# Gate projections in seven block products for eight, their tanh tiles kept in memory, the branch projections after all gates

## The chip, the cores and the metric

The kernel runs on one core of one Trainium2 chip, as one program. The metric is the device time of one execution in microseconds; where several executions were timed, the median stands for them. The core has a matrix engine (TensorE, in the profile PE, with PEld for its weight loads), a vector engine (VectorE, DVE), a scalar engine (ScalarE, ACT), a general engine (GpSimd, POOL) and a queue that issues all of this kernel's transfers (SyncE, SP). Each engine takes its instructions in the order in which they are written to it.

## The reference, cut to what matters

One decoder layer over 1024 positions of width 1024, in float32:

```python
h = rmsnorm(x, mix_norm)
q, k, v, su, sv, g_a, g_b = split(h @ w_in)
y_att = sliding_window_attention(q, k, v, ...)      # 8 heads of 64, window 128
y_sgu = gelu(su) * (tril(W_s) @ rmsnorm(gelu(sv)) + b)   # chunks of 128 positions
merged = sigmoid(g_a) * (y_att @ w_oa) + sigmoid(g_b) * (y_sgu @ w_ob)
x = x + merged @ w_out
z = causal_conv3(rmsnorm(x, ffn_norm) @ w_up)       # 2 * 2816 columns
x = x + (silu(z_gate) * z_val) @ w_down
```

`g_a` and `g_b`, the gate projections, are two products of `h` (1024 x 1024) with 1024 x 1024 weights.

## The kernel before, in words

Activations lie transposed: the feature is the partition, and the position is the free axis. Every operand of a product is split into a high part (a copy in the reduced format fp32r, made by ACT, `copy_hi`) and a low part (the rest, made by a subtraction on DVE or POOL). A product is then three matmuls: high by high, high by low, low by high. `mm3` (lines 74 to 76) writes them for dense products, `prod` (line 989) for block products.

The stages follow each other so:

1. x is loaded in eight feature tiles, and scaled and split into `hTh` and `hTl` (1024 positions in one piece from tile 2 on). The k and v projections run beside it.
2. The attention loop has 20 steps, each with hand-written places for the scores, the softmax, the transposes and the pv products, and with q, u and v-row matmuls as fillers (`FILL`). `pv_out` adds the two halves of a block's output and splits them into `yah` and `yal` (line 501).
3. The rest of the v rows (`pvs`): gelu, square and norm of each row, and its split into `vsh` and `vsl`. Here, and in the mixing products of the spatial gating unit (`sgu_mix`), a scheduler orders the instructions.
4. Gates and branches, as a list of jobs: 16 gate tiles of 48 matmuls (8 feature tiles, 2 halves, 3 products) and 16 branch tiles of 24. Jobs 0 to 2 are gates, then two gates and two branches alternate; the branches of tiles 6 and 7 come last. A gate's result is scaled, put through tanh(z/2) and held in SBUF (`th`, four buffers) until its branch multiplies it. Beside them run `sums_make` (line 825) and `sums_move`: these prepare the up projection, by loading the four quarter blocks of each pair of up weights, forming four sums, and storing all of them to memory.
5. Eight output tiles (`px`), which also split the next stage's operand into seven combinations.
6. The up projection in 22 pairs of tiles (`fast_pair`). A pair is a 2 by 2 block product in seven block products of 12 matmuls each (Winograd's form of Strassen's scheme), A11, S3, A12, S1, A22, S2, S4 by their partners. `Left` loads the weights p, q and r (r holds the sums S2 and S4, read back from memory), and splits them on ACT and POOL into `ph`/`pl`, `qh`/`ql`, `AX` and `s3h`/`s3l`. DVE forms u (line 1152), the two outputs, the scalings by the row norm, the convolution and the gated activation of the pair before; `x1` is a copy by ACT of the first product (line 1127), and the third product is added to the same PSUM bank after that copy.
7. The down projection in 7 block products of 11 slices, with the result written out.

SBUF's largest pool is `big`, with eight buffers of 16 KB per partition (`Y`). Its buffers pass from stage to stage: a new tile waits until the last reader of the old one is done. Weights come through three `raw` buffers. PSUM holds four tiles of 1024 columns (`PS`) in rotation.

Of the kernel before, what the change touches and what calls it, by code (L numbers as in the profile page):

```python
# [10 lines left out]
F = mybir.dt.float32  # L11
# [30 lines left out]
def body(ctx, tc, nc, a):  # L42
    base = ctx.enter_context(tc.tile_pool(name="base", bufs=1))
    big = ctx.enter_context(tc.tile_pool(name="big", bufs=8))
# [8 lines left out]
    def Y(s, dt=R, shape=None):  # L53
        return big.tile(shape or [128, 4, 1024], dt, tag="Y", name=nm(s))
# [40 lines left out]
    cp = base.tile([128, 186], F, name="cp")  # L95
# [26 lines left out]

    psA = ctx.enter_context(tc.tile_pool(name="psA", bufs=2, space=bass.MemoryType.PSUM, reuse_waits="tile"))
# [19 lines left out]
    hTh = [Y("hTh"), Y("hTh")]  # L143
    hTl = [Y("hTl"), Y("hTl")]
# [3 lines left out]
    def hh(k):  # L148
        return hTh[k // 4][:, k % 4, :]

    def hl(k):
        return hTl[k // 4][:, k % 4, :]
# [43 lines left out]
    xcuts = {0: (slice(0, 256), slice(256, 512), slice(512, 1024)), 1: (slice(0, 512), slice(512, 1024))}  # L196
    for k in range(8):
# [3 lines left out]
        for c in xcuts[k] if k in xcuts else (slice(0, 1024),):  # L201
            xc = x1[:, 257 + c.start:257 + c.stop]
            copy_hi(hh(k)[:, c], xc, scale=x1[:, 0:1])
            nc.vector.scalar_tensor_tensor(hl(k)[:, c], xc, x1[:, 0:1], hh(k)[:, c].bitcast(F),
                                           op0=ALU.mult, op1=ALU.subtract)
        for s in range(8):
            o = pkv[s // 4][:, (s % 4) * 256:(s % 4 + 1) * 256]
            c = slice(s * 128, (s + 1) * 128)
            mm3(o, hh(k)[:, c], hl(k)[:, c], wkv[:, 0, k, :], wkv[:, 1, k, :],
                k == 0 and s % 2 == 0, k == 7 and s % 2 == 1)  # L210
# [23 lines left out]
    def q_proj(n):  # L234
        half, b = divmod(n, 8)
        w = wq[half]
        p = PH("pq")[:, 0:256]
        c = slice(b * 128, (b + 1) * 128)
        for k in range(8):
            mm3(p, hh(k)[:, c], hl(k)[:, c], w[:, 0, k, :], w[:, 1, k, :], k == 0, k == 7)  # L240
        st[("pq", n)] = p
# [150 lines left out]
    yah, yal = Y("yah"), Y("yal")  # L392
    uT = Y("uT", F)
# [94 lines left out]
    def pv_out(n):  # L488
# [6 lines left out]
        for g in range(2):  # L495
            r = slice(64 * g, 64 * g + 64)
            nc.vector.tensor_tensor(o[r], p[r, g], o[r], op=ALU.add)
        ts_ = slice(2 * half, 2 * half + 2)
        cs = slice(b * 128, (b + 1) * 128)
        copy_hi(yah[:, ts_, cs], o)  # L500
        nc.vector.tensor_tensor(yal[:, ts_, cs], o, yah[:, ts_, cs].bitcast(F), op=ALU.subtract)
# [3 lines left out]
    def u_chunk(i):  # L505
# [4 lines left out]
        for k in (2 * j, 2 * j + 1):  # L510
            for h in range(2):
                c = slice(h * 512, (h + 1) * 512)
                mm3(p[:, c], wh[:, k, :], wl[:, k, :], hh(k)[:, c], hl(k)[:, c], k == 0, k == 7)
# [5 lines left out]
    def v_half(s, h):  # L519
# [3 lines left out]
        for k in range(8):  # L523
            mm3(pvs[s][:, 256 * h:256 * h + 256], hh(k)[:, c], hl(k)[:, c], wv[h][:, 0, k, :],
# [57 lines left out]

    assert "".join(FILL).count("u") == 16 and "".join(FILL).count("q") == 12
    man = tc.manual_schedule()
    man.__enter__()
    for n in range(20):
# [19 lines left out]
        weights(n)  # L606
        for t, p in u_done:
# [49 lines left out]

    sg_cm = tc.tile_pool(name="sg", bufs=1)
# [10 lines left out]
    with tc.issue_after(last_sel[0].ins):  # L669
# [4 lines left out]
    with tc.issue_after(last_exp[0].ins):  # L674
        for s in range(n_v[0], 4):
            v_half(s, 0)
        for s in range(8):
# [5 lines left out]
            p = pvs.pop(s)  # L683
            vg = sg.tile([128, 512], F, tag="vg", name=nm("vg"), bufs=2)
            nc.scalar.activation(vg, p, AF.Gelu_apprx_tanh, scale=rstd[:, s:s + 1])
            sq = sg.tile([128, 512], F, tag="vsq", name=nm("vsq"), bufs=1)
            ss = sg.tile([128, 1], F, tag="vss", name=nm("vss"), bufs=2)
            nc.scalar.activation(sq, vg, AF.Square, accum_out=ss)
            rsqrt_cols(ss, ss, 1, 512)
            nc.vector.scalar_tensor_tensor(vg, vg, ss[:, 0:1], sg_b, op0=ALU.mult, op1=ALU.mult)  # L690
            copy_hi(vsh[:, s, :], vg)
            nc.vector.tensor_tensor(vsl[:, s, :], vg, vsh[:, s, :].bitcast(F), op=ALU.subtract)

    psB.__exit__(None, None, None)
    psum["C"] = tc.tile_pool(name="psC", bufs=2, space=bass.MemoryType.PSUM, reuse_waits="tile")
    psC = psum["C"].__enter__()
    psum["P"] = [psC, psC, psA, psA]
    psum["H"] = None

    pools = {}  # L700
    yz = []

    def sgu_mix(t, half):
        y = yz[0]
# [13 lines left out]
        yv = y[:, t, 4 * half:4 * half + 4].rearrange("p s i -> p (s i)")  # L718
        nc.gpsimd.tensor_tensor(yv, yv, uT[:, t, 512 * half:512 * half + 512], op=ALU.mult)

    def sgu_close():
        ysh, ysl = Y("ysh"), Y("ysl")
        for t in range(4):
            yv = yz[0][:, t].rearrange("p s i -> p (s i)")
            copy_hi(ysh[:, t, :], yv)
            nc.vector.tensor_tensor(ysl[:, t, :], yv, ysh[:, t, :].bitcast(F), op=ALU.subtract)
        sg_cm.__exit__(None, None, None)
        zr_cm[0].__exit__(None, None, None)
        pools["ys"] = (ysh, ysl)
        pools["mg_cm"] = tc.tile_pool(name="mg", bufs=1)  # L730
        pools["mg"] = pools["mg_cm"].__enter__()
        pools["dr"] = ctx.enter_context(tc.tile_pool(name="dr", bufs=1, space=bass.MemoryType.DRAM))

    ms = [None] * 8
    th = {}
    jobs.clear()

    def gate(src, key):
        def main(w):
            p = PS("pg")  # L740
            dense(p, *w, hh, hl, 8)
            yield
            t = pools["mg"].tile([128, 1024], F, tag="th", name=nm("th"), bufs=4)
            nc.vector.tensor_tensor(t, p, rstd_b, op=ALU.mult)  # L744
            nc.scalar.activation(t, t, AF.Tanh, scale=0.5)
            th[key] = t
            sums_make()
            sums_move()
        jobs.append((src, 8, main))

    def branch(src, br, c):
        def main(w):
            yh, yl = (yah, yal) if br == "a" else pools["ys"]
            p = PS("po")
            dense(p, *w, lambda k: yh[:, k, :], lambda k: yl[:, k, :], 4)
            yield
            t = th.pop((br, c))
            if br == "b":
                ms[c] = pools["mg"].tile([128, 1024], F, tag=f"m{c}", name=f"m{c}")
                nc.vector.scalar_tensor_tensor(ms[c], t, 1.0, p, op0=ALU.add, op1=ALU.mult)  # L760
            else:
                nc.vector.scalar_tensor_tensor(t, t, 1.0, p, op0=ALU.add, op1=ALU.mult)
                nc.vector.tensor_tensor(ms[c], ms[c], t, op=ALU.add)
            if br == "b":
                sums_make()
                sums_move()
            if br == "b" and c == late[0]:
                mhi[:] = [Y("mh"), Y("mh")]
                mlo[:] = [Y("ml"), Y("ml")]
            for e in SPLITS.get((br, c), ()):  # L770
                m_split(e)
        jobs.append((src, 4, main))

    def m_split(c):
        copy_hi(mhi[c // 4][:, c % 4, :], ms[c])
        nc.vector.tensor_tensor(mlo[c // 4][:, c % 4, :], ms[c], mhi[c // 4][:, c % 4, :].bitcast(F),
                                op=ALU.subtract)

    mhi, mlo = [None, None], [None, None]
    late = (6, 7)  # L780
    SPLITS = {("b", 6): (0, 1, 2), ("a", 6): (3, 4), ("b", 7): (5, 6), ("a", 7): (7,)}
    gate(a["wgb"][0], ("b", 0))
    gate(a["wga"][0], ("a", 0))
    gate(a["wgb"][1], ("b", 1))
    for c in range(8):
        if c > 1:
            gate(a["wgb"][c], ("b", c))
        if c > 0:
            gate(a["wga"][c], ("a", c))
        if c not in late:  # L790
            branch(a["wob"][c], "b", c)
            branch(a["woa"][c], "a", c)

    sums = [0, None]

    def sums_move():


        i, last = sums
        if last:  # L800
            t = pools["dr"].tile([128, 4, 4, 128], F, tag=f"sum{i}", name=f"sum{i}")
            for h, (x, s3) in enumerate(last):
                ks = slice(2 * h, 2 * h + 2)
                nc.sync.dma_start(t[:, 1, ks], s3)
                nc.sync.dma_start(t[:, 0, ks], x[:, 1, 0])
                nc.sync.dma_start(t[:, 2:4, ks], x[:, 0])
# [639 lines left out]
```

## Time and profile before

| | us |
|---|---|
| median of three runs | 1255.4 (1251.83 to 1255.53) |
| the profiled execution | 1253.38 |
| its span in the profile | 1251.7 |
| TensorE busy in it | 1222.2 (98%) |
| VectorE busy | 879.7 (70%) |
| ScalarE busy | 493.5 (39%) |
| GpSimd busy | 423.9 (34%) |

The profile shows one execution. Times in it count from the span's start. A row of the timeline has the start, the duration, the engine, the line of the kernel, the operation and its tiles, and in brackets the engine's idle time before it with what ended that. A row of the windows has the busy time of each engine in a stretch, the granted TensorE clock, the share of the 16 DMA engines' time and GB/s.

### The profile page before, as it was taken

To read this page: it belongs to the slowest core of one execution; us is meant where nothing else is said; L and a number is where in the kernel's file an instruction comes from. 1 tells how busy PE (TensorE), PEld (TensorE's weight loads), DVE (VectorE), ACT (ScalarE), POOL (GpSimd) and SP (SyncE) were. 2 spreads that over 40 slices of the span, in tenths; PEclk is the share of its full clock that TensorE was granted. 3 is DMA by queue.
4 is the path that set the end of the run, shared out by engine and by line. 5 is a ranking of instruction groups with operands and counts; after the bars stand their busy time and mean duration, and the time that the engine had idled before them with its cause. 6 is when DMAs were issued, how large, how long until landed. Compare 5 with 4: busy or idle time off the path is not lost.

```text
span 1251.7 us, 16137 instructions
## 1 busy us (share of the span) xinstructions
PE 1222.2 (98%) x5962; PEld 1025.6 (82%) x5962; DVE 879.7 (70%) x1114; ACT 493.5 (39%) x773; POOL 423.9 (34%) x275
## 2 busy tenths in 40 slices
PE   7999999999999999899999999999999999999998
PEld 6878879988888888788778888888888888788887
DVE  8788896455555554767768777778777788776674
ACT  5665665421111112333434434344344353433332
POOL 5355566151222222233474354354354420000000
PEclk8999999999999999999999999999999999999999
DMA  5210003017777776535333443543533546985372
GB/s 210 82 51 19 17 18 93 1 45 247 238 238 242 244 248 225 200 118 177 126 110 138 165 150 105 175 151 126 176 125 129 176 160 201 400 276 195 116 230 87
DMA packets 114319, 194.97 MB, mean 156 GB/s; under 512 B 10944, under 2 KB 56256, under 8 KB 114240
## 3 DMA queue, kind: packets, MB, share of 16 engines
q1 hardware_dynamic: 114240, 193.94, 46.0%
q8 instruction: 47, 0.77, 0.3%
q14 instruction: 32, 0.26, 0.1%
HBM read 142.25 MB, written 51.64 MB: 155 GB/s over the span
## 4 chain that ended last, share of the span: by engine, by line
PE 79%; DVE 11%; issue 4%; DMA 2%; ACT 2%; POOL 2%; SPq 0%; POOLq 0%; DVEq 0%; ACTq 0%
PE pz L989 32%; PE pd L1268 9%; PE pdy L1268 7%; PE pg L75 4%; PE pg L74 4%; PE pg L76 4%; PE px L75 2%; PE px L76 2%; PE px L74 2%; PE po L75 2%; PE po L74 2%; PE po L76 2%; PE pvs L74 1%; PE pvs L75 1%; PE pvs L76 1%
## 5 line engine op out<-in xcount | busy, mean ns | idle before, releaser
L91 POOL TENSOR_TENSOR wjl<-wj,wjh 128x1024 fp32r<-128x1024 f32 (+1 forms) x40 | 82.9, 2074 | 231.0 <-ACT wjh L70 228.3
L70 ACT ACTIVATE wjh<-wj 128x1024 fp32r<-128x1024 f32 (+1 forms) x40 | 35.6, 889 | 211.2 <-PE pg L75 48.1
L825 DVE TENSOR_TENSOR ls<-ls 128x256 f32<-128x256 f32 x176 | 84.1, 484 | 36.0 <-DMA ls<-wup 29.4
L989 PE MATMUL pz<-T,qh 128*128 128x512 f32 x352 | 109.1, 391 | 0.0
L989 PE MATMUL pz<-B,ph 128*128 128x512 f32 x352 | 108.4, 389 | 0.0
L74 PE MATMUL pg<-hTh,wjh 128*128 128x512 f32 x256 | 99.6, 389 | 0.0
L75 PE MATMUL pg<-hTl,wjh 128*128 128x512 f32 x256 | 99.6, 389 | 0.0
L76 PE MATMUL pg<-hTh,wjl 128*128 128x512 f32 x256 | 99.6, 389 | 0.0
L954 POOL TENSOR_TENSOR s3l<-s,s3h 128x512 fp32r<-128x512 f32 x22 | 29.7, 1351 | 156.7 <-ACT s3h L70 156.7
L989 PEld LDWEIGHTS pz<-T,qh 128*128 128x128 f32 x352 | 66.3, 188 | 14.3 <-issue 0.5
L989 PEld LDWEIGHTS pz<-B,ph 128*128 128x128 f32 x352 | 66.1, 188 | 13.8
L744 DVE TENSOR_TENSOR th<-pg,rstd_b 128x1024 f32<-128x1024 f32 x16 | 19.6, 1225 | 77.8 <-PE pg L76 77.7
L994 ACT ACTIVATE tv<-pz,cp 128x1024 f32<-128x1024 f32 x22 | 26.6, 1207 | 108.0 <-DVE pz L1003 102.7
L954 POOL TENSOR_TENSOR ql<-wuq,qh 128x1024 fp32r<-128x1024 f32 x22 | 53.4, 2427 | 45.3 <-ACT qh L70 45.3
L989 PE MATMUL pz<-T,ql 128*128 128x512 f32 x176 | 68.5, 389 | 0.0
L1268 PE MATMUL pd<-bh,ah 128*128 128x512 f32 x176 | 68.5, 389 | 0.0
L1268 PE MATMUL pd<-bl,ah 128*128 128x512 f32 x176 | 68.5, 389 | 0.0
L989 PE MATMUL pz<-B,pl 128*128 128x512 f32 x176 | 68.5, 389 | 0.0
L1268 PE MATMUL pd<-bh,al 128*128 128x512 f32 x176 | 68.5, 389 | 0.0
L989 PE MATMUL pz<-T,AX 128*128 128x512 f32 x264 | 65.1, 396 | 1.0 <-DVE T L874 1.0
L989 PE MATMUL pz<-B,AX 128*128 128x512 f32 x264 | 63.4, 389 | 0.0
L989 PEld LDWEIGHTS pz<-T,AX 128*128 128x128 f32 x264 | 50.1, 191 | 11.9 <-DVE T L874 1.5
(298 smaller groups left out, 3481.3 us busy)
## 6 DMA issues: line engine op xcount, KB each, us to landing
ls<-wup SPq DMA_DIRECT2D x88, 256.0 KB, 3.5
sum<-ls SPq DMA_DIRECT2D x88, 128.0 KB, 2.2
sum<-ls SPq DMA_DIRECT2D x44, 256.0 KB, 2.3
wup<-wup SPq DMA_DIRECT2D x22, 512.0 KB, 3.9
wur<-sum SPq DMA_DIRECT2D x22, 512.0 KB, 5.2
ra<-wdown SPq DMA_DIRECT2D x44, 256.0 KB, 4.6
b<-T SPq DMA_DIRECT2D x44, 256.0 KB, 3.4
B<-tv SPq DMA_DIRECT2D x33, 256.0 KB, 2.0
```

The source lines that it names most:

```text
L70: return nc.scalar.activation(dst, src, AF.Copy, scale=scale)
L74: nc.tensor.matmul(out, wh, mh, start=first, stop=False)
L75: nc.tensor.matmul(out, wh, ml, start=False, stop=False)
L76: nc.tensor.matmul(out, wl, mh, start=False, stop=last)
L91: nc.gpsimd.tensor_tensor(l[:, :nk, :], r[:, :nk, :], h[:, :nk, :].bitcast(F), op=ALU.subtract)
L744: nc.vector.tensor_tensor(t, p, rstd_b, op=ALU.mult)
L825: nc.vector.tensor_tensor(o, p, q, op=op)
L954: nc.gpsimd.tensor_tensor(l, r, h.bitcast(F), op=ALU.subtract)
L989: nc.tensor.matmul(o, p[:, k, :], y[:, q, k, :], start=not more and k == 0 and j == 0, stop=k == 3 and j == 2, skip_group_check=True)
L994: nc.scalar.activation(t, z, AF.Identity, scale=cw[:, ci, 2:3], bias=cb[:, ci:ci + 1])
L1268: nc.tensor.matmul(o[d], p[:, k - k0, m], q[:, k - k0, :], start=new and k == 0 and j == 0, stop=k == HK - 1 and j == 2, skip_group_check= ...
```

## The change

It is one rewrite with these parts.

- The gate projections of feature tile c, `g_b` and `g_a`, become one pair (`gate_pair`) in the seven-product form of the up projection. A pair has 84 matmuls where its two gate tiles had 96. The seven combinations of x (`xb`: B11, B21, B22, T1 to T4) are formed once. B11, B21 and B22 are the quarter blocks of the split x that exist already, which is why x is now split in halves of 512 positions from tile 0 on (`hx`). For the four others x is loaded again (`rows_again`), scaled by ACT (`x_gain`), summed by DVE (`x_sums`) and split (`x_split`). The weights' sums S1 to S4 are formed on DVE (`sums_q`, `sums_r`).
- All gates come before all branches. The tanh tiles are stored to memory (`gate_out`) and loaded again two branches ahead (`th_load`). Branches run in the order b0 b1 a0 a1 b2 b3 a2 a3 and so on.
- The attention output `ya` is stored to memory unsplit, and loaded and split beside the last gate pairs (`ya_load`, `ya_split`). The spatial unit's output is split in the last pair (`ys_split`).
- From the v rows on everything is written in order by hand (`v_phase`). The first half of the mixing products moves in among the last v rows. Seven of the large buffers have tag Y, and one has a tag of its own, U.
- The up weights' sums stored ahead shrink to S3 and S1 (`sums_step`). In the up pairs S2 and S4 are formed by two DVE subtractions (`sums_r`) instead of being loaded, and their split (`split_r`) moves behind that of q.
- Job weights are loaded four jobs ahead instead of three.

The diff, cut to its core:

```diff
+    def x_gain(r, ks):
+        for k in ks:
+            x = xr_raw[r][:, k, :]
+            nc.scalar.activation(x, x, AF.Copy, scale=cp[:, 186 + 4 * r + k:187 + 4 * r + k])
...
+        if n == 15:
+            rows_again(0)
+        if n == 17:
+            x_gain(0, (0, 1))
+        if n == 18:
+            x_gain(0, (2, 3))
+            x_sums((0, 1), True)
+        if n == 19:
+            x_sums((2, 3), True)
...
+    rows_again(1)
...
-            job_load(i + 3)
+            job_load(i + 4)
...
+    X_WORK = {
+        0: lambda: g_left[0].split_p(),
+        1: lambda: x_gain(1, (0, 1)),
+        2: lambda: (x_gain(1, (2, 3)), x_sums((0, 1), False)),
+        3: lambda: x_sums((2, 3), False),
+        4: first_sums,
+    }
+    def v_phase():
...
+        g_left[0].load_p()
+        g_left[0].load_q()
...
+            if s > 0:
+                v_norm(s - 1)
+            if s > 5:
+                sgu_mix(s - 6, 0)
+            v_gelu(s)
+            if s in X_WORK:
+                X_WORK[s]()
+            v_rsqrt(s)
+            if s > 0:
+                v_split(s - 1)
...
+        def sums_r(self):
+            self.r = raw("lr")
+            s2 = sub(nc.vector, self.r[:, 0:4], self.q[:, 0:4], self.p[:, 0:4])
+            sub(nc.vector, self.r[:, 4:8], self.p[:, 4:8], s2)
...
+    def gate_out(key, z):
+        t = pools["ls"].tile([128, 1024], F, tag="th", name=nm("th"), bufs=3)
+        nc.scalar.activation(t, z, AF.Tanh, scale=0.5)
+        d = d_th[key] = pools["dr"].tile([128, 1024], F, tag=f"th{key}", name=nm("dth"))
+        nc.sync.dma_start(d, t)
...
+    def gate_pair(c, prev):
...
+        q.prod(q.g0, "A11", "B11")
...
+        nc.scalar.copy(x1, q.g0)
+        if prev:
+            gate_out(("b", c - 1), prev.zg)
+            sums_step()
+        else:
+            w.split_s3()
+            sgu_mul(0, 1)
+            x_split("T1")
+            w.split_q()
+            for t in (1, 2, 3):
+                sgu_mul(t, 1, nc.vector)
+            x_split("T4")
+            q.prod(q.g0, "A12", "B21", more=True)
+        q.prod(q.v0, "S3", "T3")
+        nc.scalar.copy(x7, q.v0)
+        if not c:
+            w.split_r()
+            x_split("T2")
+        else:
+            q.prod(q.g0, "A12", "B21", more=True)
+        if nx:
+            nx.sums_q()
+            nx.split_p()
+            nx.split_s3()
...
+        q.prod(q.g1, "S1", "T1")
+        nc.vector.tensor_tensor(x7, x7, q.g1, op=ALU.add)
+        if nx:
+            nx.sums_r()
...
+        q.prod(q.v0, "A22", "T4", more=True)
+        if nx:
+            nx.split_q()
...
+        q.prod(q.v1, "S2", "T2")
+        nc.vector.tensor_tensor(q.u2, x1, q.v1, op=ALU.add)
+        nc.vector.tensor_tensor(q.v0, q.u2, q.v0, op=ALU.add)
+        nc.vector.tensor_tensor(q.v1, q.u2, x7, op=ALU.add)
+        q.scale(q.zv)
...
+        gate_out(("a", c), q.zv)
+        q.prod(q.g1, "S4", "B22", more=True)
...
         prev.stores()
+        if nx:
+            nx.sums_r()
         if n + 2 < NPAIR:
             lefts[n + 2].load_p()
         q.prod(q.v0, "A22", "T4", more=True)
         if nx:
             nx.split_q()
+            nx.split_r(n + 1)
```

More of the change, by code (lines that the diff above doesn't have):

```diff
@@ L496, in pv_out @@
             r = slice(64 * g, 64 * g + 64)
[L497 to L501, printed above, removed]
+            nc.vector.tensor_tensor(ya[r, 2 * half:2 * half + 2, b * 128:(b + 1) * 128], p[r, g], o[r], op=ALU.add)
+        if b == 7:
+            for t in (2 * half, 2 * half + 1):
+                nc.sync.dma_start(d_ya[t], ya[:, t, :])
     ust = {("w", 0): tuple(u_next)}
@@ L682, in body @@
                 nc.scalar.activation(uT[:, s, :], uT[:, s, :], AF.Gelu_apprx_tanh)
[L683 to L700, printed above, removed]
+            if s > 0:
[8 more added lines that the diff above has]
+                v_split(s - 1)
+        v_norm(7)
+        v_split(7)
+        sgu_mix(2, 0)
+        sgu_mix(3, 0)
+    pools = {"dr": dr}
     yz = []
     def sgu_mix(t, half):
+        if not yz:
+            yz.append(Y("y", F, [128, 4, 8, 128]))
         y = yz[0]
@@ new lines, in body, with sums_load, sums_step @@
+    sums = {"load": 0, "make": 0}
+    def sums_load():
+        i = sums["load"]
+        if i < NPAIR:
+            x = pools["ls"].tile([128, 3, 4, 128], F, tag="ls", name=nm("ls"), bufs=2)
+            nc.sync.dma_start(x[:, 0], a["wup"][2 * i][:, 0:4])
+            nc.sync.dma_start(x[:, 1:3], a["wup"][2 * i + 1].rearrange("p (b k) m -> p b k m", b=2))
+            sums[i] = x
+            sums["load"] += 1
+    def sums_step():
+        i = sums["make"]
+        if i < NPAIR:
+            sums_load()
+            x = sums.pop(i)
+            sub(nc.vector, x[:, 0], x[:, 0], x[:, 1])
+            sub(nc.vector, x[:, 1], x[:, 1], x[:, 2], ALU.add)
+            t = pools["dr"].tile([128, 2, 4, 128], F, tag=f"sum{i}", name=f"sum{i}")
+            nc.sync.dma_start(t, x[:, 0:2])
+            pools.setdefault("sum", {})[i] = t
+            sums["make"] += 1
@@ new lines, in ya_split, with gates, th_load @@
+    def ya_split():
+        for t in range(4):
+            y_split("a", t, yb["raw"][:, t, :])
+    def gates():
+        q = None
+        for c in range(8):
+            q = gate_pair(c, q)
+        q.last_sum()
+        gate_out(("b", 7), q.zg)
+        gates_close()
+        for key in B_ORDER[:2]:
+            th_load(key)
+    B_ORDER = [(br, c + e) for c in range(0, 8, 2) for br in "ba" for e in (0, 1)]
+    ms = {}
+    def th_load(key):
+        th[key] = pools["ls"].tile([128, 1024], F, tag="th", name=nm("th"), bufs=3)
+        nc.sync.dma_start(th[key], d_th[key])
@@ L780, in body @@
[L780 to L806, printed above, removed]
-            pools.setdefault("sum", {})[i] = t.rearrange("p b k m -> p (b k) m")
-            i += 1
-        sums[:] = [i, None]
-        if i < NPAIR:
-            sums[1] = []
-            for h in range(2):
-                x = pools["mg"].tile([128, 2, 2, 2, 128], F, tag=f"ls{h}", name=nm("ls"))
-                s3 = pools["mg"].tile([128, 2, 128], F, tag=f"ls3{h}", name=nm("ls3"))
-                for t in range(2):
-                    nc.sync.dma_start(x[:, t], a["wup"][2 * i + t].rearrange("p (b k) m -> p b k m", b=2)
-                                      [:, :, 2 * h:2 * h + 2])
-                sums[1].append((x, s3))
@@ L840, in body @@
+    for n in range(16):
+        branch(n)
     comb = {}
@@ L1366, in body @@
     jobs.append((None, 0, None))
-    yz.append(zr[0].tile([128, 4, 8, 128], F, tag="Z", name="y"))
-    for i in range(3):
-        job_load(i)
-    job_split(0)
-    for half in range(2):
-        for t in range(4):
-            sgu_mix(t, half)
-    sgu_close()
-    with tc.manual_schedule():
-        job_split(1)
+    with tc.manual_schedule():
+        v_phase()
+        psB.__exit__(None, None, None)
+        psum["C"] = tc.tile_pool(name="psC", bufs=2, space=bass.MemoryType.PSUM, reuse_waits="tile")
+        psC = psum["C"].__enter__()
+        psum["P"] = [psC, psC, psA, psA]
+        psum["H"] = None
+        for t in range(4):
+            sgu_mix(t, 1)
+        x_split("T3")
+        for t in range(4):
+            sgu_mul(t, 0)
+        sg_cm.__exit__(None, None, None)
+        gates_open()
+        g_left[1].load_p()
+        gates()
         run_jobs()
```

359 lines of the change are left out of this document (221 added, 138 removed).

## The prediction

> **What bounds the kernel now.** I read the busy table, then the windows by stage, then TensorE's timeline.
>
> ```profile
> span 1251.7 us, 16137 instructions
> PE 1222.2 (98%) x5962; PEld 1025.6 (82%) x5962; DVE 879.7 (70%) x1114; ACT 493.5 (39%) x773; POOL 423.9 (34%) x275
> ```
>
> ```profile
> 200.00:237.00 37.00, 37.00 (x313) 37.00 (x312) 18.69 (x26) 19.05 (x36) 15.00 (x14) 1.00 0.21 65
> 237.00:256.00 19.00, 17.48 (x145) 17.10 (x144) 11.50 (x19) 5.91 (x12) 7.12 (x7) 1.00 0.00 1
> 256.00:500.00 244.00, 244.00 (x1081) 202.11 (x1080) 128.99 (x211) 45.15 (x49) 61.88 (x34) 1.00 0.68 221
> 640.00:1036.00 396.00, 396.00 (x1749) 327.90 (x1748) 306.15 (x313) 169.27 (x189) 169.75 (x81) 1.00 0.44 149
> ```
>
> TensorE (the first busy column) never rests in the gates and branches (256 to 500) or in the up pairs (640 to 1036). There only fewer matmuls, or a new wait, can change the time. A matmul's 389 ns is not its price, since its successor starts earlier:
>
> ```profile
> 329.92 0.39 PE L74 MATMUL pg<-hTh,wjh 128*128 128x512 f32 x1
> 332.64 0.39 PE L74 MATMUL pg<-hTh,wjh 128*128 128x512 f32 x1
> ```
>
> ```profile
> 630.98 405.32 PE pz L989 x1788
> ```
>
> Between the two gate rows lie twelve steps in 2.72 us, 0.2267 us each. The up projection, which is already done in seven products, steps at 405.32 / 1788 = 0.2267 too, so seven-product matmuls are no slower. For the 256-column matmuls of the v rows, 37.00 us / 313 gives 0.118.
>
> **The gate products: -21.8.** Before, 16 gate tiles take 48 matmuls each, 768. After, 8 pairs take 7 x 12 = 84 each, 672. The 96 that go are worth 96 x 0.2267 = 21.8 us. The branches keep their 384.
>
> What each steady pair adds must fit in 84 x 0.2267 = 19.0 us. DVE gets thirteen 512-wide operations of 0.69 and two 1024-wide of 1.23 (rows of 824.18 and 816.58 below): 11.4 us. POOL gets three splits of 2.40 and one of 1.31. DMA moves two weight tiles, two tanh stores, two sum loads and two sum stores, 4.6 MB, which is 242 GB/s against 221 at a 0.68 share now. All fit, so I take nothing; if this cover were gone, DMA would be first. The tanh stores stand on SP's queue in front of the next weights, for about 2 us of a pair that has 13 us before these are needed.
>
> **Attention: -2.** The branch output is no longer split there, so `yal` (DVE) and its high copy (ACT) go; the rows also show how DVE and POOL exclude each other.
>
> ```profile
> 98.00:208.00 110.00, 106.76 (x688) 92.97 (x689) 92.32 (x193) 72.05 (x220) 68.69 (x78) 0.97 0.08 25
> ```
>
> ```profile
> L501 DVE TENSOR_TENSOR yal<-o,yah x16: 425/832/2434, 99.1 to 213.6; 128x256 fp32r<-128x256 f32 x16
> ```
>
> ```profile
> 209.54 2.41 POOL L673 TENSOR_TENSOR wgl<-s,wgh 128x1024 fp32r<-128x1024 f32 x1 [1.18 <-ACT wgh L70]
> 209.80 2.43 DVE L501 TENSOR_TENSOR yal<-o,yah 128x256 fp32r<-128x256 f32 x1 [1.52 <-ACT yah L70]
> 212.25 0.86 DVE L497 TENSOR_TENSOR o<-pv,o 64x256 f32<-64x256 f32 x2
> 615.79 2.40 POOL L954 TENSOR_TENSOR AX<-wur,AX 128x1024 fp32r<-128x1024 f32 x1 [8.00 <-ACT AX L70]
> 617.22 5.53 DVE L874 TENSOR_TENSOR T<-T2f,T 128x512 fp32r<-128x512 f32 x4 [0.54 <-ACT T L70]
> 618.15 2.84 POOL L954 TENSOR_TENSOR ql<-wuq,qh 128x1024 fp32r<-128x1024 f32 x1
> ```
>
> TensorE waits only 110 - 106.76 = 3.2 us in this loop, so relieving DVE of 16 operations of about 0.8 can bring at most that. The halves of x (six more instructions on ACT and on DVE), two x sums and four gain copies that are put here cost some of it. Bounds -3 to +1; I take -2.
>
> **The v rows: +5.** A DVE operation with both inputs in SBUF waits out a POOL operation: `yal` needs 0.43 alone and took 2.43 beside `wgl`. This matters for what is now written in a fixed order. The steps:
>
> ```profile
> 8.00:14.00 6.00, 3.11 (x24) 2.71 (x22) 6.00 (x3) 6.00 (x9) 5.84 (x3) 1.00 0.96 390
> ```
>
> ```profile
> x<-ac SPq DMA_DIRECT2D x8, 512.0 KB, 2.7
> ```
>
> ```profile
> 203.65 1.06 ACT L682 ACTIVATE uT<-uT 128x1024 f32<-128x1024 f32 x1
> 208.75 0.28 PE L74 MATMUL pvs<-wvB,hTh 128*128 128x256 f32 x1
> 219.89 0.67 ACT L685 ACTIVATE vg<-pvs,rstd 128x512 f32<-128x512 f32 x1
> 220.01 0.69 DVE L692 TENSOR_TENSOR vsl<-vg,vsh 128x512 fp32r<-128x512 f32 x1 [0.70 <-ACT vsh L70]
> 220.59 0.63 ACT L688 ACTIVATE vsq<-vg 128x512 f32<-128x512 f32 x1
> 245.63 0.39 PE L74 MATMUL pm<-wgh,vsh 128*128 128x256 f32 x1 [1.11 <-ACT vg L685]
> 252.06 0.36 PE L74 MATMUL pm<-wgh,vsh 128*128 128x256 f32 x1 [0.41 <-DVE y L716]
> 256.45 0.40 PE L74 MATMUL pg<-hTh,wjh 128*128 128x512 f32 x1
> ```
>
> `rows_again(1)` needs a buffer of tag Y; counting those alive (four x tiles, `ya`, `wv`, the first raw x), it gets the one that `ya` leaves once stored. The last adds (212.25 now) come without `yal`'s 1.52 + 2.43 at about 208.3; the two stores land near 211.5. Behind them on SP's queue stand four x rows, `rb` and the first gate weights, 6 x 0.52 MB, 8.1 us at 390 GB/s; they land about 221.5. ACT meets `split_p` of these weights right after row 0's gelu, at 213, and stops there for 8 us. Queued behind it: that copy (1.06), two gelus of u (1.06), two rows of gelu, square and its accumulator read (1.5), two gains (1.06), one split: 8.5 us, so row 2's PSUM half comes free at 230. TensorE, six half rows of 24 x 0.118 after 208.75, wants it at 225.7 and waits 4.2. At the end row 7 runs through gelu, square, power, norm and split (some 4.5 us with handoffs) behind 1.4 us of adds on DVE, against three mixes of 12 x 0.118: a wait of 2.6, where it is now 1.11 + 0.41. Together +5; nothing if the weights land by 217, +9 at 250 GB/s.
>
> **The first two pairs: +8.5.** Pair 0 begins while its operands are still being split. After the last mix DVE has about 2.1 us of adds and nineteen two-input operations of 0.69 before T2 is whole: 15.2 us. POOL has, on the same port, S3's split, one product with u and the splits of q and r:
>
> ```profile
> 249.92 1.74 POOL L719 TENSOR_TENSOR y<-y,uT 128x512 f32<-128x512 f32 x1 [2.35 <-DVE y L716]
> ```
>
> 1.31 + 1.74 + 2.40 + 2.40 = 7.9 us. The rows of 615.79 to 618.15 show the two taking turns, each waiting for the other. In series that is 23.1 us, then the last quarter of S2 and all of S4 (3.4): 26.5 against 19.0, +7.5; with POOL wholly beside DVE it would be 0. I take 7, nearer the rows, and 1.5 for pair 1, whose first copy ACT reaches late.
>
> The Trainium skill (SBUF — State Buffer, Who interferes with whom) says that a VectorE instruction with two SBUF inputs and a GpSimd one that reads SBUF exclude each other for the whole instruction. The rows agree: 2.43 for 0.43 of work. The rule speaks against this change.
>
> **Gates to branches to output: -2.5.** Two waits go, since the output weights are asked for one job earlier, tanh tiles arrive two branches ahead and `m` is split as it is made:
>
> ```profile
> 521.14 0.50 PE L76 MATMUL px<-mh,wjl 128*128 128x512 f32 x1 [2.55 <-POOL wjl L91]
> 531.45 0.50 PE L75 MATMUL px<-ml,wjh 128*128 128x512 f32 x1 [0.72 <-DVE ml L776]
> ```
>
> These are 3.3 us; after the last branch add, copy and split (about 5 us) must beat the eighth slice of the first output tile at 9.5, so what is late next is not TensorE. The first tanh tiles land some 3 us after their branch ends; four PSUM tiles cover that. Bounds -3.3 to +2.
>
> **Clock: +1.5.** A wait can leave slow steps behind it:
>
> ```profile
> 175.09 0.80 PE L74 MATMUL pu<-hTh,wuh 128*128 128x512 f32 x1 [1.68 <-DVE uT L608]
> 175.69 0.63 PE L75 MATMUL pu<-hTl,wuh 128*128 128x512 f32 x1
> 176.11 0.63 PE L76 MATMUL pu<-hTh,wul 128*128 128x512 f32 x1
> ```
>
> Steps of 0.42 follow this wait, 0.2 too many for about eight matmuls; after the wait of 2.55 the clock stayed full. Between 0 and four times 1.6; I take one.
>
> **The up pairs: 0.** S2 and S4 are now made by two DVE operations (`sums_r`) instead of a load.
>
> ```profile
> 805.14 0.69 DVE L1152 TENSOR_TENSOR u<-x,pz 128x512 f32<-128x512 f32 x1 [3.59 <-PE pz L989]
> 816.58 1.23 DVE L1023 SCALAR_TENSOR_TENSOR pz<-pz,tg 128x1024 f32<-128x1024 f32 x1 [1.16 <-ACT pz L1020]
> 819.58 0.99 DVE L869 TENSOR_TENSOR tv<-tv,tv 128x512 f32<-128x512 f32 x1
> 822.42 2.40 POOL L954 TENSOR_TENSOR ql<-wuq,qh 128x1024 fp32r<-128x1024 f32 x1 [2.40 <-ACT qh L70]
> 824.18 0.69 DVE L1152 TENSOR_TENSOR u<-x,pz 128x512 f32<-128x512 f32 x1 [2.28 <-PE pz L989]
> 829.62 0.59 ACT L1127 COPY x<-pz 128x512 f32<-128x512 f32 x1 [0.78 <-PE pz L989]
> ```
>
> The two operations (1.4 us) fall into the wait of 2.28 or 3.59 before `u`. If `ql` comes between them, `u` is 1 to 2 us late. That delays the scaling, ACT's tap and then its copy of x1 (829.62), which must be done one product (2.72) after it became possible: 2.72 - 0.59 - 0.2 = 1.9 us are free. Bounds 0 to 8.
>
> **Sum.** -21.8 - 2 + 5 + 8.5 - 2.5 + 1.5 + 0 = -11.3. The profiled execution took 1253.4 us (span 1251.7 and 1.7 around it): 1242.1. The median before is 1255.4, 2.0 above that execution; I add half of this: 1243.
>
> **Rivals.** *The cover holds*: the weights land before ACT asks, v rows +0, first pairs +4, no clock term: 1233. For it: POOL's and ACT's idle shares; against it: the fixed order.
>
> *The port makes DVE the bound in the up pairs* (slower). Two pairs leave DVE 2.28 + 3.59 + 2 x 1.16 = 8.2 us idle. `sums_r` takes 2.8; if in each pair both `pl` and `ql` stand in front of a DVE operation for 2.4 each, 9.6 more are lost: 4.2 us over per two pairs, 10.5 times: 1243 + 44 = 1287. It decides from 2.7 us of waits a pair, and passes before's time at 1.1 us lost per two pairs. For it: 819.58 took 0.99 instead of 0.69; against it: that is 0.3, not 2.4. By the rule that the Trainium skill gives (above), every meeting costs the rest of the POOL operation, which would make this rival's price the upper one.
>
> *The second x half gets `wv`'s buffer, not `ya`'s*: free only after the last first-half row, about 230; everything behind on SP slips by 18 us: 1260.
>
> *The products don't shrink the stage*, because a DMA of 242 GB/s with in-order waits paces each pair at the old 21.8: 1264. Against it: 390 GB/s above.
>
> **Numbers.** Forecast 0.63, cover holds 0.19, port 0.09, wrong buffer 0.06, DMA pace 0.03. A measurement of this kernel tells about 0.3% (3.8 us) from no change. Faster by more than that (below 1251.6): 0.60 of the forecast's 0.63, all of the cover case, 0.03 of a mild port case: 0.82. Same: 0.07. Slower: 0.11. The terms' bounds give the forecast 1236 to 1252; with the cover case and mild port losses the range is 1231 to 1256, leaving out about 0.18.
>
> **What would show it.** TensorE records fall by 96; the eight pairs take 19.0 us each from the second or third on; a wait of about 4 us of `pvs` on ACT near 226; waits on T1, T4, T2 in pair 0; none at the first output tile; up pairs still 19.04. It is wrong if the up pairs lengthen, if waits recur in every gate pair, or if the v rows wait over 10 us.

## The result and the profile after

| | before | after |
|---|---|---|
| median, us | 1255.5 (1251.83 to 1258.36) | 1285.2 (1283.31 to 1286.94) |
| ratio | | 1.0238 (95% interval 1.0208 to 1.0269) |
| profiled execution, us | 1253.4 | 1285.6 |
| its span, us | 1251.7 | 1283.8 |

The changed kernel is 2.4% slower; 1243 was forecast. The head of its page, the chain of work that ended last (shares of the span), and the group that stands second by cost:

```profile
span 1283.8 us, 15830 instructions
PE 1216.0 (95%) x5866; PEld 1013.6 (79%) x5866; DVE 1032.4 (80%) x1127; ACT 530.3 (41%) x823; POOL 457.4 (36%) x288
PE 54%; DVE 32%; ACT 6%; issue 5%; DMA 2%; POOL 1%; SPq 0%; ACTq 0%; DVEq 0%; POOLq 0%
L888 PE MATMUL pz<-B,ph 128*128 128x512 f32 x352 | 116.1, 412 | 30.2 <-ACT x L1323 30.2
```

TensorE has 96 matmuls fewer (5962 before), as it should, yet it is busy for 95% of the span instead of 98%. VectorE is busy 153 us longer (879.7 before) and holds 32% of the chain (11% before). One group of matmuls waited 30.2 us in all for ScalarE's copy x1. These are the up pairs; the windows by stage say so too. First the stretch that the prediction shows of before (640 to 1036), then the parts ahead of it: v rows, gates, branches, output tiles.

```profile
640.00:1036.00 396.00, 367.66 (x1571) 298.99 (x1570) 363.49 (x316) 150.27 (x169) 161.88 (x75) 0.98 0.30 104
```

```profile
205.24:252.30 47.06, 45.58 (x387) 45.00 (x386) 31.44 (x53) 25.64 (x44) 13.54 (x13) 1.00 0.22 79
252.30:420.30 168.00, 158.23 (x673) 127.63 (x673) 148.54 (x138) 64.72 (x83) 74.87 (x34) 0.98 0.64 218
420.30:507.40 87.10, 87.10 (x386) 72.09 (x385) 52.76 (x52) 19.29 (x25) 20.67 (x15) 1.00 0.75 274
507.40:594.40 87.00, 87.00 (x385) 72.05 (x384) 57.77 (x49) 26.59 (x34) 31.68 (x17) 1.00 0.39 142
```

TensorE was never idle in the up pairs of before. Now it lacks 28 of 396 us there, and VectorE (third busy column) is at 92% instead of 77%. Branches and output tiles have no gap.

The length of the up pairs is read from the first and the last of the 21 adds `u`, one in each pair; 20 pairs lie between them. Timeline, VectorE; before, then after:

```profile
652.82 0.69 DVE L1152 TENSOR_TENSOR u<-x,pz 128x512 f32<-128x512 f32 x1 [1.43 <-PE pz L989]
1033.62 0.69 DVE L1152 TENSOR_TENSOR u<-x,pz 128x512 f32<-128x512 f32 x1 [1.44 <-PE pz L989]
```

```profile
638.31 0.69 DVE L1349 TENSOR_TENSOR u<-x,pz 128x512 f32<-128x512 f32 x1 [1.75 <-PE pz L888]
1062.94 0.68 DVE L1349 TENSOR_TENSOR u<-x,pz 128x512 f32<-128x512 f32 x1
```

That makes 380.80 us before (19.04 a pair), 424.63 after (21.23 a pair): 43.8 us more. At the first `u` the changed kernel is 14.5 us ahead (638.31 against 652.82); at the last it is 29.3 behind. The stages add up to the whole difference of the spans:

| stretch | before | after | difference | forecast |
|---|---|---|---|---|
| up to the last v rows | 208.75 | 205.24 | -3.5 | -2 |
| v rows and mixing | 47.7 | 47.06 | -0.6 | +5 |
| gates, branches, output tiles | 352.45 | 342.1 | -10.3 | -14.3 |
| first up pairs, up to the first `u` | 43.92 | 43.90 | 0 | |
| 20 up pairs | 380.80 | 424.63 | +43.8 | 0 |
| the rest | 218.08 | 220.86 | +2.8 | 0 |

Why the up pairs grew can be read in one pair. Timeline after, all engines, other rows left out:

```profile
676.68 2.84 POOL L853 TENSOR_TENSOR ql<-lq,qh 128x1024 fp32r<-128x1024 f32 x1
677.19 2.88 DVE L597 TENSOR_TENSOR lr<-lq,lp 128x512 f32<-128x512 f32 x1
680.10 0.69 DVE L597 TENSOR_TENSOR lr<-lp,lr 128x512 f32<-128x512 f32 x1
...
681.43 0.70 DVE L1350 TENSOR_TENSOR pz<-u,pz 128x512 f32<-128x512 f32 x1
681.96 2.39 POOL L853 TENSOR_TENSOR AX<-lr,AX 128x1024 fp32r<-128x1024 f32 x1 [2.45 <-ACT AX L75]
682.16 2.75 DVE L1351 TENSOR_TENSOR pz<-u,x 128x512 f32<-128x512 f32 x1
...
686.21 1.20 ACT L1195 ACTIVATE tv<-pz,cp 128x1024 f32<-128x1024 f32 x1 [4.32 <-DVE pz L892]
687.32 0.57 ACT L1323 COPY x<-pz 128x512 f32<-128x512 f32 x1
687.94 0.73 PE L888 MATMUL pz<-B,ph 128*128 128x512 f32 x2 [1.57 <-ACT x L1323]
```

The first subtraction of `sums_r` starts beside GpSimd's split `ql` and ends only after it: 2.88 us where its twin takes 0.69. Then AX, now split behind `ql`, covers the add `v1` (`pz<-u,x`): 2.75. The add one row above it, with one operand in PSUM, takes 0.70. Behind `v1` stand the scaling, ScalarE's tap, its copy x1, and the third product, which waits. The groups by form give the whole run's sums for `v1` and for the adds of the stores, before and after:

```profile
L1154 DVE TENSOR_TENSOR pz<-u,x 128x512 f32<-128x512 f32 x21 | 14.7, 699 | 0.7
L869 DVE TENSOR_TENSOR tt<-tv,tt 128x512 f32<-128x512 f32 x22 | 15.1, 686 | 0.4
```

```profile
L1351 DVE TENSOR_TENSOR pz<-u,x 128x512 f32<-128x512 f32 x21 | 54.0, 2572 | 0.7
L597 DVE TENSOR_TENSOR tt<-tv,tt 128x512 f32<-128x512 f32 x22 | 36.5, 1657 | 0.4
```

`v1` has grown by 39.3 us and the store adds by 21.4, without a change in what either computes.

### The profile page after: what moved, and what is told of

Read it like the earlier page. It is cut to its first block, busy times and chain, and to the rows that moved or that the text cites. A ratio compares the mean times of both kernels' runs of the same rounds, so it can differ in the third digit from the quotient of the medians.

```text
span 1283.8 us, 15830 instructions
## 1 busy us (share of the span) xinstructions
PE 1216.0 (95%) x5866; PEld 1013.6 (79%) x5866; DVE 1032.4 (80%) x1127; ACT 530.3 (41%) x823; POOL 457.4 (36%) x288
## 4 chain that ended last, share of the span: by engine, by line
PE 54%; DVE 32%; ACT 6%; issue 5%; DMA 2%; POOL 1%; SPq 0%; ACTq 0%; DVEq 0%; POOLq 0%
PE pz L888 14%; PE pdy L1465 7%; PE pd L1465 7%; DVE pz L1351 4%; DVE tv L1200 3%; DVE tg L1200 3%; DVE lr L597 3%; DVE pz L892 2%; PE px L81 2%; PE po L81 2%; PE po L79 2%; PE px L80 2%; PE px L79 2%; PE po L80 2%; DVE tt L597 2%
## 5 line engine op out<-in xcount | busy, mean ns | idle before, releaser
L888 PE MATMUL pz<-T,qh 128*128 128x512 f32 x480 | 148.9, 391 | 1.1 <-ACT x L980 1.1
L888 PE MATMUL pz<-B,ph 128*128 128x512 f32 x352 | 116.1, 412 | 30.2 <-ACT x L1323 30.2
L853 POOL TENSOR_TENSOR pl<-lp,ph 128x1024 fp32r<-128x1024 f32 x30 | 72.9, 2430 | 111.6 <-ACT ph L75 111.6
L888 PEld LDWEIGHTS pz<-T,qh 128*128 128x128 f32 x480 | 90.1, 188 | 21.4 <-ACT x L980 1.5
L888 PE MATMUL pz<-T,ql 128*128 128x512 f32 x240 | 93.6, 390 | 0.0
L853 POOL TENSOR_TENSOR ql<-lq,qh 128x1024 fp32r<-128x1024 f32 x30 | 81.5, 2718 | 20.7 <-ACT qh L75 20.7
L96 POOL TENSOR_TENSOR wjl<-wj,wjh 128x512 fp32r<-128x512 f32 (+1 forms) x24 | 40.6, 1690 | 109.3 <-ACT wjh L75 109.3
L892 DVE TENSOR_TENSOR pz<-pz,rstd_b 128x1024 f32<-128x1024 f32 x60 | 74.0, 1233 | 2.1
L888 PE MATMUL pz<-T,s3h 128*128 128x512 f32 x240 | 74.1, 390 | 0.3 <-ACT x L1268 0.3
L853 POOL TENSOR_TENSOR AX<-lr,AX 128x1024 fp32r<-128x1024 f32 x22 | 52.7, 2395 | 53.6 <-ACT AX L75 53.6
L597 DVE TENSOR_TENSOR ls<-ls 128x512 f32<-128x512 f32 x44 | 57.8, 1314 | 0.8
L888 PEld LDWEIGHTS pz<-B,AX 128*128 128x128 f32 x264 | 49.6, 188 | 10.3
```

Source lines behind the costliest of these rows:

```text
L96: nc.gpsimd.tensor_tensor(l[:, :nk, :], r[:, :nk, :], h[:, :nk, :].bitcast(F), op=ALU.subtract)
L597: eng.tensor_tensor(out, x, y, op=op)
L853: nc.gpsimd.tensor_tensor(l, r, h.bitcast(F), op=ALU.subtract)
L888: nc.tensor.matmul(o, p[:, k, :], y[:, q, k, :], start=not more and k == 0 and j == 0, stop=k == 3 and j == 2, skip_group_check=True)
L892: nc.vector.tensor_tensor(z, z, rstd_b, op=ALU.mult)
```

## The experiments

Three theories were to be told apart. **Port**: a VectorE operation with two SBUF operands and a GpSimd split exclude each other, and the change put two such meetings into each pair: `v1` beside AX's split, and beside `ql` either the first subtraction of `sums_r` or an add of the stores. **Work**: the 1.4 us of `sums_r` per pair are simply too much for VectorE. **ScalarE order**: AX's high copy now stands ahead of the tap and of x1 on ScalarE. "us a pair" below is the mean of the 20 pairs, from the first and the last `u` of each kernel as above.

| kernel | base | median, us | ratio to before (95%) | us a pair |
|---|---|---|---|---|
| r_from_memory | after | 1280.2 | 1.021 (1.0187 to 1.0233) | 19.10 |
| before_r_late | before | 1254.4 | 1.0003 (0.9984 to 1.0022) | 19.05 |
| v1_from_psum | after | 1262.8 | 1.0074 (1.0051 to 1.0097) | 20.19 |
| sums_at_tanh | after | 1239.9 | 0.9884 (0.9862 to 0.9905) | 19.10 |
| split_r_own_pair | after | 1249.1 | 0.9929 (0.9899 to 0.9959) | 19.46 |
| two_tanh_buffers | sums_at_tanh | 1244.6 | 0.9908 (0.9877 to 0.9939) | 19.10 |
| tanh_late_ya | sums_at_tanh | 1236.8 | 0.9846 (0.9821 to 0.987) | 19.10 |
| before_4_psum | before | 1266.9 | 1.0082 (1.0059 to 1.0105) | 19.57 |
| before_4_sbuf | before | 1299.3 | 1.0341 (1.0311 to 1.0371) | 20.96 |

**S2 and S4 from memory again.**

The edit, cut; the first part is in `sums_step`, the rest in `fast_pair`:

```diff
+            sub(nc.vector, x[:, 1], x[:, 0], x[:, 1], ALU.add)
+            sub(nc.vector, x[:, 0], x[:, 2], x[:, 0])
+            sub(nc.vector, x[:, 2], x[:, 1], x[:, 2])
+            sub(nc.vector, x[:, 3], x[:, 3], x[:, 2])
...
+            nx.load_r()
...
+            nx.split_r(n + 1)
         prev.tanh()
...
-            nx.sums_r()
...
-            nx.split_r(n + 1)
```

> In the up pairs S2 and S4 are loaded again (formed with S3 and S1 in the gate and branch stages), and their split stands ahead of the tanh as before. To make room the tanh tiles have two buffers instead of three. Three theories of the 447.00 us that the up pairs took (405.3 before). Port: VectorE operations with two SBUF operands stand behind GpSimd's splits, the add v1 (2.76 instead of 0.70) beside AX, sums_r and the adds of the stores (2.88 to 3.6) beside ql. Work: it is only the 1.4 us more of VectorE per pair. ScalarE order: AX's copy now stands in front of the next pair's tap and of x1. All three expect the window of the up pairs to fall back to 404 to 408 us and a time of 1239 to 1250 (two buffers for the tanh tiles may cost some us in gates and branches). If the window stays above 430, the loss is not in how S2 and S4 are made.

The up pairs were back at 19.10, so the loss was in how S2 and S4 are made and split. But the whole took 1280, 30 us over the expected range, since the loss had moved ahead: 182.7 us in the gates instead of 168.0, 102.2 in the branches instead of 87.1, and 95.3 in the output tiles instead of 87.0. The gate pairs show why; timeline of this kernel:

```profile
316.20 1.28 DVE L597 TENSOR_TENSOR lr<-lq,lp 128x512 f32<-128x512 f32 x1
317.51 2.85 DVE L597 TENSOR_TENSOR lr<-lp,lr 128x512 f32<-128x512 f32 x1
320.29 2.86 DVE L597 TENSOR_TENSOR ls<-ls 128x512 f32<-128x512 f32 x4
323.06 0.68 DVE L1017 TENSOR_TENSOR u<-x,pz 128x512 f32<-128x512 f32 x1
...
329.05 0.73 PE L892 MATMUL pz<-x,ph 128*128 128x512 f32 x2 [1.70 <-ACT x L972]
```

Gate pairs form sums on VectorE beside splits as well. Four `ls` adds instead of two, twice a pair, leave no room ahead of `u`, and x1 is late by 1.70 in pair after pair: 21.13 a pair (waits at 307.92, 329.05, 350.19 and 371.32). So loading the sums is cheap only where the four adds have room; here they had none.

**AX's split moved alone, in the kernel before.**

```diff
-        if nx:
-            nx.split_r()
         prev.tanh()
...
             nx.split_q()
+            nx.split_r()
```

> The kernel before with one step moved: split_r behind split_q, so that AX is split beside the add v1; S2 and S4 are still loaded, no sums_r. Port: v1 takes 2.7 instead of 0.7 in nearly every pair, but 2 x 2.06 us per two pairs fit into the 8.2 us that VectorE is idle there: 1255 to 1260, window 405 to 410. ScalarE order: AX's copy (1.06) in front of tap and x1 costs about 1 us a pair, 21 times: 1277. Work: no more work, 1255.

No change, and TensorE has no wait in the up pairs at all. The place of AX's copy on ScalarE, taken alone, is ruled out as the cause. The meetings are there nevertheless; groups of this kernel:

```profile
L1153 DVE TENSOR_TENSOR pz<-u,x 128x512 f32<-128x512 f32 x21 | 36.3, 1729 | 0.7
L869 DVE TENSOR_TENSOR tt<-tv,tt 128x512 f32<-128x512 f32 x22 | 35.9, 1633 | 0.4
```

Some 42 us more of VectorE's time than in the kernel before cost nothing, because they fit into its waits ahead of `u`: 57.7 us in the kernel before, 19.0 here. A meeting is not yet a loss.

**v1 without a second SBUF operand.**

```diff
-        nc.vector.tensor_tensor(q.v1, q.u2, x7, op=ALU.add)
+        nc.vector.tensor_tensor(q.v1, x1, q.v1, op=ALU.add)
+        nc.vector.tensor_tensor(q.v1, x7, q.v1, op=ALU.add)
```

> The kernel after, but v1 is formed by two adds that each have one operand in PSUM (x1 + the product, then + x7) instead of one add of two SBUF tiles: 0.70 us more VectorE work per pair, nothing on the shared port. Port: each of the two takes 0.70 beside AX's split, 1.40 instead of 2.76: 1.36 less per pair, 21 times = 28 us: 1257 (1250 to 1264), window 420. Work: 0.70 more per pair, 21 times = 15 us: 1300. ScalarE order: 1285, no change.

Two instructions instead of one made the kernel 22.4 us faster; by the theory of work it would have become slower. Timeline:

```profile
660.56 2.40 POOL L853 TENSOR_TENSOR AX<-lr,AX 128x1024 fp32r<-128x1024 f32 x1 [2.45 <-ACT AX L75]
660.75 0.69 DVE L1351 TENSOR_TENSOR pz<-x,pz 128x512 f32<-128x512 f32 x1
661.48 0.69 DVE L1352 TENSOR_TENSOR pz<-x,pz 128x512 f32<-128x512 f32 x1
```

Both run at full speed in the middle of AX's split, where the single add took 2.76. The gain over the 20 pairs is 20.8 us, less than was worked out: the single add had a mean of 2.57, not 2.76 (groups above; 2.67 in the 20 pairs), which makes 1.29 a pair, 25.7. What took the other 5 was not looked for.

**sums_r where VectorE waits for the tanh.**

```diff
         if nx:
             nx.split_s3()
+            nx.sums_r()
         nc.scalar.copy(x7, q.v0)
...
         prev.stores()
-        if nx:
-            nx.sums_r()
```

> The kernel after with sums_r moved from behind the stores to between the taps and the tanh's reader, where VectorE waits 1.16 us for the tanh and no split of q runs; AX's split stays behind ql, so v1 still meets it. Port: sums_r takes 1.4 instead of 2.9 to 3.6, v1 stays at 2.76; 2 x (2.06 + 1.4 - 1.16) and what the stores still lose lie under the 8.2 us idle: window 405 to 412, 1240 to 1250. Work: 2.8 more per two pairs less 2.3 of tanh wait: 0.5 x 10.5 = 5 us over 1243, 1248. ScalarE order: AX's copy keeps its place in front of the tap and x1: 1280 to 1286.

As the port theory had it: 1239.9, at the lower edge of its range, and 45.3 us less than the changed kernel, from one step moved. Timeline:

```profile
668.36 0.68 DVE L597 TENSOR_TENSOR lr<-lq,lp 128x512 f32<-128x512 f32 x1
668.53 1.03 ACT L1214 ACTIVATE pz<-tg 128x1024 f32<-128x1024 f32 x1 [2.86 <-DVE tg L1200]
669.08 0.69 DVE L597 TENSOR_TENSOR lr<-lp,lr 128x512 f32<-128x512 f32 x1
669.68 1.23 DVE L1217 SCALAR_TENSOR_TENSOR pz<-pz,tg 128x1024 f32<-128x1024 f32 x1
```

`sums_r` is done while ScalarE computes the tanh; the operation after it starts without a wait. `v1` met AX only in part: a mean of 1.78 in the 20 pairs, where 2.76 was expected. This run alone does not separate port from work, since the work is hidden too.

**S2 and S4 split in the pair that uses them.**

```diff
+        lefts[n].split_r(n)
         prev.tanh()
...
             nx.split_q()
-            nx.split_r(n + 1)
```

> The kernel after with sums_r at its place behind the stores, beside the split of q, but S2 and S4 split one pair later, in the pair that uses them, ahead of the tanh; so no split of AX runs beside the add v1. Port: v1 takes 0.70 instead of 2.76, 2.06 less per pair; sums_r still takes 2.9 to 3.6. Worked through in order with the rows' durations, 4.1 less per two pairs brings the pairs back to 19.0 to 19.6 us: 1237 to 1252. Work: nothing is taken away, 1285, or 1240 only if the order on ScalarE mattered. ScalarE order: before_r_late has ruled it out, but AX's copy stands where it stood before, so this theory too would give 1240; the row of v1 and the waits of x1 tell the two apart.

It took 1249.1, and 19.46 a pair, inside the port's range. `sums_r` has kept its place and its work, and `v1` is free of AX. Groups; the first holds the gate pairs as well (in the 20 up pairs alone the mean is 1.84 us):

```profile
L597 DVE TENSOR_TENSOR lr<-lq,lp 128x512 f32<-128x512 f32 x30 | 48.6, 1619 | 0.0
L1350 DVE TENSOR_TENSOR pz<-u,x 128x512 f32<-128x512 f32 x21 | 14.7, 699 | 0.7
```

So either meeting can be taken out and nearly all of the time comes back. The two together exceed what VectorE has free ahead of `u`.

**The tanh buffers alone.**

```diff
-        t = pools["ls"].tile([128, 1024], F, tag="th", name=nm("th"), bufs=3)
+        t = pools["ls"].tile([128, 1024], F, tag="th", name=nm("th"), bufs=2)
...
-                th_load(B_ORDER[n + 2])
+                th_load(B_ORDER[n + 1])
```

> sums_at_tanh (1239.9) with two buffers for the tanh tiles instead of three and tanh tiles loaded one branch ahead, as r_from_memory had them. It tells which part of r_from_memory's loss in gates and branches (182.7 instead of 167.2 us, and 102.2 instead of 87.0) comes from the buffers and which from two more adds a pair on VectorE. If VectorE and the port: gates stay at 167 to 169, branches 87 to 103, 1240 to 1256. If the buffers: gates 180 or more, 1270.

It took 1244.6, with 167.8 in the gates and 89.7 in the branches. The buffers explain 2.7 of the 15 us that r_from_memory lost in the branches and none of what it lost in the gates. The other 12 in the branches went with more sums and larger transfers there; which of these was not told apart.

**The attention rows fetched one pair later.**

```diff
-        if c == 5:
+        if c == 6:
             ya_load()
```

> sums_at_tanh with the attention rows asked back in gate pair 6 instead of 5, so that the last gate pair's weights no longer queue behind 2 MB on SP; the wait of 2.13 us for x1 in pair 7 (405.35 there) should go: 1.5 to 3 us less, 1237 to 1238.5. If the rows then come too late for the first branch, a wait of up to 4 us at the first branch and 1242.

It took 1236.8, with 165.4 in the gates instead of 167.2. It is the fastest of all kernels here and beats the kernel before by 1.5%. Its interval overlaps that of sums_at_tanh, so the last 3 us are not shown to be its own.

**Four scratch adds in the kernel before: one operand in PSUM, or none.**

```diff
         prev.stores()
+        ex = ft.tile([128, 512], F, tag="ex", name=nm("ex"))
+        for _ in range(4):
+            nc.vector.tensor_tensor(ex, x7, q.g1, op=ALU.add)
```

The second kernel has `x1` in the place of `q.g1`.

> The kernel before with four more VectorE adds in each up pair behind the stores, twice as many as sums_r has; each reads one operand from PSUM and one from SBUF and writes a scratch tile that nothing reads. It doubles the work and leaves the port alone. Work: 2.8 us a pair, 5.6 per two pairs against 8.2 idle; what VectorE's order leaves uncovered, by the same share that sums_r lost in the changed kernel (2.2 us a pair for 1.4 of work), would be 4.4 a pair, 21 times = 92: 1345. Port: the adds fit into the waits ahead of u of 2.28 and 3.59 us and of 1.16 for the tanh: 19.04 a pair, 1255 to 1262.

> The same four adds, but both operands from SBUF. Nothing else differs from the kernel with a PSUM operand. Port: one of them stands about 2.2 us behind the split of q in each pair, and an add of the stores behind that of p: worked through in order 20.8 us a pair, 20 times 1.8 = 36 more: 1285 to 1295. Work: as with a PSUM operand, no difference between the two kernels.

The same instruction, the same count, the same place; only the home of one operand differs: 1266.9 against 1299.3. Groups, first from PSUM, then from SBUF:

```profile
L1146 DVE TENSOR_TENSOR ex<-x,pz 128x512 f32<-128x512 f32 x84 | 57.5, 684 | 2.2
```

```profile
L1146 DVE TENSOR_TENSOR ex<-x,x 128x512 f32<-128x512 f32 x84 | 79.4, 945 | 2.2
```

With SBUF operands, a pair took 20.96 against an expected 20.8; the whole lies 4.3 us above its range, and in its trace 2.8 us were lost ahead of the edited pairs, where the two kernels are alike. With PSUM, a pair took 19.57 against an expected 19.04: that expectation missed by 10.6 us over the 20 pairs, and 1266.9 lies 4.9 above its range. TensorE waited 7.2 us for `ex` itself there, since its adds read a bank into which the last product is added; the rest is presumably VectorE having used up its room. The kernel with SBUF operands has no such wait, so the difference between the two is, if anything, too small. Twice the work of `sums_r` cost 0.5 us a pair, the port another 1.4.

## Why the prediction was wrong, step by step

**The up pairs, 0: the step that failed**, and alone more than the whole error. Its sentence was that the two operations "fall into the wait of 2.28 or 3.59 before `u`", or `u` comes 1 to 2 us late if `ql` stands between them. It looked at the work that was added and not at the split that was moved. It names neither `v1`, which reads `u` and x7, both in SBUF, nor the move of AX behind `ql`, so that this move stood at nothing without a reason. Measured, `v1` loses up to 2.06 us a pair beside AX, and `sums_r` or the stores 2.2 beside `ql`, besides 1.4 of work. VectorE's waits over the whole run (us in all, times, longest), before and then after, and the two operations of `sums_r` between the first and the last `u` show why this did not fit:

```profile
DVE u L1152 <- PE pz L989: 57.7, 21, 3.6
DVE pz L1023 <- ACT pz L1020: 26.7, 21, 3.3
```

```profile
DVE u L1349 <- PE pz L888: 6.8, 5, 1.7
DVE pz L1217 <- ACT pz L1214: 24.3, 21, 1.2
```

```profile
L597 DVE TENSOR_TENSOR lr<-lq,lp 128x512 f32<-128x512 f32 x19 | 21.7, 1143 | 0.0
L597 DVE TENSOR_TENSOR lr<-lp,lr 128x512 f32<-128x512 f32 x19 | 15.4, 808 | 0.7
```

VectorE has 39.3 us more on `v1`, 21.4 more on the store adds and 37.1 on `sums_r`: 97.8. The waits ahead of `u` took in 57.7 - 6.8 = 50.9 of it. The waits for the tanh took in almost nothing, since none of the new work stands ahead of the operation that waits there. So some 47 us are left over, and 43.8 were measured; the sum of durations is a little too large, as rows that follow each other overlap slightly.

**The port rival**, chance 0.09, came out nearly exact: 1287 against 1285.2, and 4.2 us per two pairs against 4.4. It had the mechanism right, but named `pl` and `ql`; it was `ql` and AX. That its number fits so well is in part luck. It booked 9.6 us of waiting per two pairs, where the rows give some 7 ((39.3 + 21.4 + 10.9) / 10, the 10.9 being the 37.1 of `sums_r` less 38 operations at 0.69), and set 8.2 us idle against it, of which 2.3 were the tanh's and could not be used. What was held against it, one add that took 0.99 instead of 0.69, was a row of the old order. There AX was split from 815.26 to 817.67, beside the operation at 816.58, which has an operand in PSUM and took its usual 1.23. The Trainium skill (SBUF — State Buffer, Who interferes with whom) says that a VectorE instruction with at most one SBUF input, outside the modes that use both ports, does not contend with GpSimd, and that one with two SBUF inputs contends with a GpSimd instruction that reads SBUF. The runs agree: 0.69 beside AX with one, 2.75 with two. Applied to each instruction behind the moved split, that rule would have given `v1` away.

**Ahead of the up pairs** the forecast was -11.3 and the run gave -14.5, so with `sums_r` moved the kernel lands at 1239.9, near the 1243. That this is so near is in part luck, since its terms missed in both directions:

- The products: 96 matmuls fewer, as counted, and pairs 2 to 6 run without a wait.
- Attention, -2: -3.5 came out, just past its bound of -3; it was not taken apart.
- v rows, +5: measured -0.6. What failed here is the queue's order. It was read off the written code; the trace has the gate weights issued ahead of the stores of `ya`, and ScalarE splits them at 209.65 with no wait ahead of it. Why the queue's order is not the written one is not shown. The queue's rows:

```profile
192.70 0.33 SPq L85 DMA_DIRECT2D lp<-wgb  x1
197.94 0.33 SPq L85 DMA_DIRECT2D lq<-wga  x1
205.78 0.80 SPq L505 DMA_DIRECT2D ya<-ya  x2
```

- First two gate pairs, +8.5 and clock, +1.5: the gates took 168.0 us against 8 x 19.04 = 152.3. Of the 15.7 over, 7.1 are waits in pairs 0 and 1, as on these rows, 2.7 one wait in pair 7 that was not foreseen, and 5.9 are steps longer than 0.2267. Of these, 1.7 fall on the twelve matmuls behind the wait at 257.02 (4.43 us for them) and 1.6 on the eight behind the one at 275.38, together twice what was taken for the clock; the other 2.6 are spread over the stage and were not taken apart:

```profile
257.02 0.73 PE L888 MATMUL pz<-x,ph 128*128 128x512 f32 x2 [1.86 <-ACT x L966]
...
275.38 3.56 PE L888 MATMUL pz<-T,gax 128*128 128x512 f32 x8 [1.81 <-DVE T L742]
278.77 2.94 PE L888 MATMUL pz<-x,gax 128*128 128x512 f32 x12
...
406.50 0.73 PE L888 MATMUL pz<-x,ph 128*128 128x512 f32 x2 [2.68 <-ACT x L966]
```

- Gates to branches to output, -2.5: the two waits are gone, and no new one came.
- The rivals of DMA pace and of the wrong buffer: neither happened. Branches and output tiles ran at full step with TensorE busy throughout.
- After the up pairs, 0: +2.8. The last wait of the down projection's start grew from 1.60 to 3.37; its cause was not pursued.

## What to carry to other kernels

When a step moves on GpSimd, list every VectorE instruction that it will now run beside and look at where its operands live: those with two in SBUF waited here until the split had ended, and an added instruction may be the smaller part of the cost. Compare the sum of these waits and of the new work, over the pattern's full period, with the idle time that VectorE has behind them in its own order: here the waits ahead of `u` counted, and those for the tanh did not until `sums_r` stood ahead of them (24.3 us of them in the changed kernel, 1.2 with it moved). Each of two meetings alone was nearly free (19.05 and 19.46 us a pair), and both together cost 2.2 us a pair. New work goes where VectorE already waits for another engine and GpSimd is idle.

## What the runs showed of the hardware that was not expected

An add that writes to PSUM is not safe from the port: `v1` writes PSUM and still took 2.75, because both inputs are in SBUF. Two adds with one PSUM operand each (0.69 + 0.69) beat one with none (2.76) beside a split.

The length of a wait does not tell whether TensorE goes on slowly behind it. Behind the wait of 1.81 us at 275.38 eight matmuls take 3.39 us to the next row (278.77), 0.424 each instead of 0.2267, and behind the 1.86 at 257.02 there are slow steps too; the granted clock was 0.72 from 272.60 to 278.77. Behind the longer wait of 2.68 at 406.50, and behind 2.92 in an up pair, the steps are the usual ones:

```profile
710.20 0.72 PE L888 MATMUL pz<-B,ph 128*128 128x512 f32 x2 [2.92 <-ACT x L1323]
...
713.07 0.61 PE L888 MATMUL pz<-T,qh 128*128 128x512 f32 x2
```

Twelve matmuls start from the first of these rows up to the second, in 2.87 us. What decides was not shown.
